# A two-layer transformer block with routed experts: the block plan and its branch ahead of the token lists, gMLP products on VectorE, and a fixed order of adds at the layers' ends

## The chip, the cores and the metric

The kernel runs on one core of a Trainium2 chip. The metric is the device time of one execution in microseconds, the median of the runs shown. Compute engines are TensorE (PE in the profile; its weight loads are PEld), VectorE (DVE), ScalarE (ACT) and GpSimd (POOL); SyncE (SP) issues most of the weight transfers.

## The reference, cut to what matters

512 latent tokens and 256 context tokens of width 1024 pass two layers. Layer 0 mixes tokens by windowed attention, layer 1 by a chunked gMLP; each is followed by a norm, a mixture of 16 experts (two per token, both of one group of four experts), and a second norm. The residual stream stays in float32.

```python
# layer 1's mixer
z = gelu(h @ w_in + b_in); u, v = z[..., :1024], z[..., 1024:]
v = layer_norm(v, ln_g, ln_b).reshape(B, n, 128, 8, 128)
s = einsum("gpq,bnqgc->bnpgc", w_s, v) + b_s
y = (u * s.reshape(B, L, 1024)) @ w_out
x = layer_norm(ALPHA * x + g_a * y, ...)
# after either mixer, for h = modulate(x, sh_f, sc_f)
s = sigmoid(h @ router_w)             # 16 scores per token; the best two of the best group
y[t] = sum over the two: gate * (silu(h @ w1[e]) * (h @ w3[e])) @ w2[e]
x = layer_norm(ALPHA * x + g_f * y, ...)
```

The modulation vectors (shift, scale and gate, twice per layer) come from a product of silu(c) with a 1024 x 6144 matrix per layer.

## The kernel before, in words

Weights stream from memory in pieces of 128 x 1024 floats, 512 KB each. One list, `pieces`, holds them in the order of use; `issue(n)` asks for all of them up to place n on the SP queue, into one pool of 28 buffers (`slot`); `adv` after each use moves `issue` on. The planner that orders the instructions of each engine works with estimated times; it takes program order as priority, may place a step ahead of others written before it, and is told otherwise by `issue_after`, by `high_priority` (what stands inside goes first) and by `in_order` (the steps of the named engines keep the order in which they are written).

The kernel's stages follow one another: modulation vectors and projections, attention, output projection with norm and routing (`mix_out`, `route`), the first MoE (`moe(0, ...)`), the last norm of layer 0, the gMLP, `mix_out` and `route` of layer 1, the second MoE, and the last norm with the stores of the output.

A MoE stage works on units: blocks of 128, 64 or 32 rows of one expert, 28 in layer 0 and 22 in layer 1, in groups of 128 rows. The first two experts of each layer are fixed (the last two of the 16), so their 24 pieces are asked for ahead; the order of the other 14 depends on the counts of tokens. `plan` (L860 to L898) ranks the experts by their counts and writes the numbers into `R["int"]`, from which SP reads where to fetch from (`fetch`, L224). It also counts the blocks that don't fit (`R["int"][:, NR:]`): `more` reads that count into a register of every engine and branches around an overflow part. `places` and `slots` make lists of tokens by one-hot columns on VectorE (L997) and small matmuls (L974); `gather` fetches the rows of one group by such a list from the GpSimd queue (L1008), and `to_xT` transposes them on TensorE (L1019). A unit is then `gemm1` (L1045), `glu` (L1055, L1056), `to_hT` (L1065), `gemm2` (L1078), and `store`, which writes the scaled rows to memory (`ydr`). At unit n - 2 `collect` gathers, for each token tile, its two rows from `ydr` (L1116). The last two units don't pass through memory: their rows reach the tokens by a matmul with one-hot columns (`rows` in `last_norm`, L695).

In `moe` the order around the change is: list and gather of group 0, plan, places, lists of groups 1 to 3, gathers 1 and 2, the branch (`more`), transposes of group 0, units. `combine` (L1124) adds the gathered rows to the residual stream: X = y * gate + X, on 128 x 1024 tiles, all four tiles of the second choice in the last unit and all four of the first behind it. `last_norm` then adds the matmuls' rows with row sums (L703), squares on ScalarE (L710) and takes a Newton square root (`newton`, L737 to L753) for two tiles at a time. In layer 0 the normalised tiles go to `pre` (transposes at L1341) and into the gMLP's v half (`vhalf`, `vnorm`), then a loop over eight column blocks f for u; there the second half of layer 1's modulation matrix (16 pieces of "mt", rows 32 to 47) is multiplied in `gemt`, two pieces per f. In this loop every other product is on VectorE (L368) and the rest on GpSimd with a ScalarE sum (L370, L371). At the kernel's end ScalarE scales, VectorE multiplies with the norm's g, GpSimd or VectorE adds b, and SP stores. Weights that are used as two float32r halves (`KSPLIT`) are split by a ScalarE cast (L229) and a VectorE subtraction (L230).

## Time and profile before

| | |
|---|---|
| median of 3 runs | 1188.14 us (1185.77 to 1191.42) |
| the profiled execution | 1186.24 us |
| its span, first to last instruction | 1184.4 us |
| PE / PEld busy | 1014.6 us (86%) / 589.6 us (50%) |
| DVE / ACT / POOL busy | 611.5 us (52%) / 359.9 us (30%) / 271.2 us (23%) |
| mean granted TensorE clock | 0.925 |
| DMA | 330.62 MB, mean 279 GB/s |

Busy times are sums of an engine's instructions; matmul ends are modelled, so a busy PE need not be at its peak. The page's 40 slices (29.6 us each) give the course: the first MoE fills slices 13 to 22, the second 30 to 38 (counted from 0).

```
PE   5799899996992999999999399599929999999980
DVE  1798988785457621221122896876565121221247
POOL 0044333323000123231213251410001221120131
PEclk7799999998996999999999799799959999999995
DMA  9934457547274999999998316365449999898991
```

### The profile page before, as it was taken

What the parts mean: (1) busy time and instruction counts of PE and PEld (TensorE: products, weight loads), DVE (VectorE), ACT (ScalarE), POOL (GpSimd) and SP (SyncE); (2) the same over time, 40 slices, a digit from 0 to 9 for tenths busy, and PEclk for the clock granted to TensorE, in tenths of its full rate; (3) what the DMA queues carried; (4) which work ended last, traced back from release to release, by engine and by line L of the source; (5) the groups of instructions that cost most, each with busy time, mean ns of one, the idle gap of its engine ahead of it and who ended that gap; (6) DMA issues with size and microseconds to landing.
All of it is one profiled execution on the core that took longest, in us unless ns stands there. A gap on an engine that the chain in (4) does not pass through costs nothing. (4 is left out here: it accounts for less than half of the span.)

```text
span 1184.4 us, 18461 instructions
## 1 busy us (share of the span) xinstructions
PE 1014.6 (86%) x6596; PEld 589.6 (50%) x6596; DVE 611.5 (52%) x1548; ACT 359.9 (30%) x730; POOL 271.2 (23%) x262
## 2 busy tenths in 40 slices
PE   5799899996992999999999399599929999999980
PEld 2577665554782444444443178488713342444420
DVE  1798988785457621221122896876565121221247
ACT  1553487775312111111121343442212110111103
POOL 0044333323000123231213251410001221120131
PEclk7799999998996999999999799799959999999995
DMA  9934457547274999999998316365449999898991
GB/s 346 408 148 174 157 196 258 173 145 256 102 269 160 377 409 390 410 410 409 410 386 324 118 46 244 131 212 203 178 189 387 410 411 410 311 407 352 386 382 71
DMA packets 104284, 330.62 MB, mean 279 GB/s; under 512 B 13346, under 2 KB 24306, under 8 KB 104179
## 3 DMA queue, kind: packets, MB, share of 16 engines
q1 hardware_dynamic: 88608, 287.56, 63.4%
q0 software_dynamic: 10848, 26.75, 6.0%
q10 hardware_dynamic: 4722, 14.98, 3.5%
q8 instruction: 56, 0.92, 0.3%
q14 instruction: 50, 0.40, 0.1%
HBM read 310.72 MB, written 21.67 MB: 281 GB/s over the span
## 5 line engine op out<-in xcount | busy, mean ns | idle before, releaser
L1045 PE MATMUL pb<-ring,xt 128*32 128x256 f32 (+1 forms) x2112 | 228.1, 440 | 1.1 <-DMA ring<-in_moe 0.8
L1045 PEld LDWEIGHTS pb<-ring,xt 128*32 128x32 f32 (+1 forms) x2112 | 86.7, 117 | 114.9 <-issue 70.4
L1089 POOL DMA_DIRECT2D ydr<-ys x132 | 67.0, 513 | 319.2 <-DVE ys L1084 258.9
L1056 DVE TENSOR_TENSOR si<-si,pb 128x128 f32<-128x128 f32 (+1 forms) x46 | 16.1, 350 | 206.9 <-ACT si L1055 203.4
L370 POOL TENSOR_TENSOR raw<-raw,row 128x1024 f32<-128x1024 f32 x32 | 90.8, 2850 | 131.8 <-DMA raw<-in_mt 104.5
L1078 PE MATMUL pb<-ring,hh 128*32 128x256 f32 (+1 forms) x1056 | 119.5, 441 | 1.7 <-ACT hh L1067 0.8
L368 DVE SCALAR_TENSOR_TENSOR raw<-raw,row 128x1024 f32<-128x1024 f32 x48 | 83.6, 1760 | 4.1 <-DMA row<-sdr 4.1
L1055 ACT ACTIVATE si<-pb 128x128 f32<-128x128 f32 (+1 forms) x46 | 15.1, 329 | 219.4 <-PE pb L1045 219.4
L1078 PEld LDWEIGHTS pb<-ring,hh 128*32 128x32 f32 (+1 forms) x1056 | 43.0, 117 | 62.5 <-issue 45.8
L1084 DVE TENSOR_TENSOR ys<-pb,gfs 128x256 f32<-128x256 f32 (+1 forms) x42 | 22.6, 537 | 81.5 <-PE pb L1078 79.9
L1008 POOL DMA_INDIRECT xg<-hdr,Rgi x22 | 23.3, 1057 | 178.6 <-DVE pq L887 87.7
L230 DVE TENSOR_TENSOR wl<-raw,wh 128x1024 fp32r<-128x1024 f32 x44 | 53.8, 1247 | 15.3 <-ACT wh L229 15.2
L1067 ACT COPY hh<-pt 128x128 f32<-128x128 f32 (+2 forms) x50 | 17.0, 339 | 146.1 <-PE pt L1065 139.4
L569 DVE TENSOR_SCALAR_CACHE_REDUCE P<-pa,nsink 128x512 f32<-128x512 f32 (+1 forms) x64 | 50.5, 809 | 19.7 <-PE pa L565 10.9
L1045 PE MATMUL pa<-ring,xt 128*128 128x512 f32 x128 | 59.4, 604 | 0.6 <-DVE xt L1027 0.6
L571 ACT ACTIVATE P<-P,nm 128x512 f32<-128x512 f32 (+1 forms) x64 | 49.5, 775 | 11.9 <-DVE P L569 11.6
L605 ACT COPY PT<-pt 128x512 f32<-128x512 f32 x72 | 39.4, 582 | 27.2 <-PE pt L604 27.0
L604 PE MATMUL pt<-cc,P 128*128 128x128 f32 x288 | 43.9, 281 | 4.1 <-ACT PT L605 3.5
L229 ACT CAST wh<-raw 128x1024 fp32r<-128x1024 f32 x44 | 44.5, 1044 | 8.7 <-DMA mdr<-gr 6.9
L604 PEld LDWEIGHTS pt<-cc,P 128*128 128x128 f32 x288 | 31.0, 141 | 31.0 <-issue 25.2
L1025 ACT ACTIVATE xt<-pt,bc,gc 128x128 f32<-128x128 f32 x88 | 33.1, 457 | 38.2 <-PE pt L1019 20.9
L614 PE MATMUL pb<-PT,Vt 128*64 128x512 f32 x144 | 38.8, 617 | 3.6 <-ACT PT L605 3.6
(368 smaller groups left out, 2005.0 us busy)
## 6 DMA issues: line engine op xcount, KB each, us to landing
ring<-in_moe SPq DMA_DIRECT2D x336, 512.0 KB
raw<-in_mt SPq DMA_DIRECT2D x80, 512.0 KB
raw<-in_moe SPq DMA_DIRECT2D x48, 512.0 KB
raw<-in_mod SPq DMA_DIRECT2D x16, 512.0 KB
raw<-in_qkv SPq DMA_DIRECT2D x12, 512.0 KB
ydr<-zero SPq DMA_DIRECT2D x10, 512.0 KB
ydr<-ys POOLq DMA_DIRECT2D x36, 128.0 KB, 5.6
raw<-in_wo SPq DMA_DIRECT2D x8, 512.0 KB
```

Of the source, the lines that this page charges most:

```text
L229: SC.copy(hi, src)
L230: V.tensor_sub(lo, src, hi.bitcast(F32))
L368: V.scalar_tensor_tensor(w, w, 1.0, srow[0], op0=OP.mult, op1=OP.mult, accum_out=mv[l][:, j:j + 1])
L370: GP.tensor_mul(w, w, srow[0])
L569: V.tensor_scalar(P[j], reg, -0.125, nsink[:, p * 8 + j:p * 8 + j + 1], op0=OP.mult, op1=OP.min, accum_out=nm[:, j:j + 1])
L571: SC.activation(P[j], P[j], AF.Exp, bias=nm[:, j:j + 1], scale=-1.0, accum_out=sums[:, j:j + 1])
L604: PE.transpose(pt[:, j * 128:(j + 1) * 128], P[a * 4 + j][:, i * 128:(i + 1) * 128], idf)
L605: cp = SC.copy(tl[:, a, :], pt)
L614: m.append(PE.matmul(po[a * 64:(a + 1) * 64, :], Vt[kb // 3][:, kb % 3, g * 64:(g + 1) * 64], tl[:, a, :], start=(i == 0), stop=(i == nb - ...
L1045: PE.matmul(o.rearrange("p (m c) -> p m c", m=2), xt[:, k, c:c + n], w[:, h], start=(k == 0), stop=(k == 7), skip_group_check=True)
L1078: PE.matmul(o, ht[f], w[:, h], start=(f == 0), stop=(f == 3), skip_group_check=True)
L1089: GP.dma_start(ydr[row:row + n, h * n * 8:(h + 1) * n * 8], ys[h * n:h * n + n, :])
```

## The change

1. `moe`: the plan stands under `high_priority`; `places`, the lists of groups 1 to 3 and the gathers 1 and 2 stand behind the branch and behind the transposes of group 0.
2. Pieces: winv 0 to 3 come ahead of the last 16 pieces of the first MoE, and are split at unit n - 2; `issue` looks 4 pieces further from the 160th on.
3. gMLP: all late products of `gemt` are on VectorE, behind the norm of v's last tile, spread by LATE over f = 1 to 7; their row (`srow`) is loaded right behind the first MoE.
4. `last_norm`: written out in a fixed order on TensorE, VectorE and ScalarE. The first choice's rows of tiles 2 and 3 are added by matmuls with a diagonal matrix of gates instead of `combine`; `combine` takes a range of tiles. Layer 0 takes the first pair's norm ahead of the last tile's sums; layer 1 takes one norm for four tiles, multiplies with g ahead of it, and works on VectorE alone, but for tile 1, whose last step is a matmul onto b with a diagonal of scales.

```diff
-    pieces += moe_pieces(0)
-    pieces += [("winv", j) for j in range(8)] + [("ws",)]
+    first = moe_pieces(0)
+    pieces += first[:-16] + [("winv", j) for j in range(4)] + first[-16:]
+    pieces += [("winv", j) for j in range(4, 8)] + [("ws",)]
+    LATE = [0, 0, 3, 6, 8, 10, 12, 14, 16]
     for j in range(8):
-        pieces += [("winu", j), ("mt", 1, 32 + 2 * j), ("mt", 1, 33 + 2 * j)]
+        pieces += [("winu", j)] + [("mt", 1, 32 + i) for i in range(LATE[j], LATE[j + 1])]
...
-    def gemt(l, j):
+    def gemt(l, j, past=None):
         w = raw("mt", l, j)
-        if (j % 4 != 3 if l and j < 32 else j % 2):
-            V.scalar_tensor_tensor(w, w, 1.0, srow[0], op0=OP.mult, op1=OP.mult, accum_out=mv[l][:, j:j + 1])
+        if past or (j % 4 != 3 if l else j % 2):
+            m = V.scalar_tensor_tensor(w, w, 1.0, srow[0], op0=OP.mult, op1=OP.mult, accum_out=mv[l][:, j:j + 1])
+            if past:
+                after(m, past)
...
+        def scaled(u, p):
+            V.scalar_tensor_tensor(ys[u], p, R["gs"][:, u:u + 1], gf, op0=OP.mult, op1=OP.mult)
+            for t in range(4):
+                rows(t, u, ys[u])
         with in_order(PE, V, SC):
...
+            scaled(0, R["py"])
+            combine(l, 1, X, 0, 2)
+            scaled(1, py)
+            for t in (2, 3):
+                for n in range(2):
+                    PE.matmul(o[t][n], dg[t - 2], R["y", t, 0][:, n * 512:n * 512 + 512], start=False, stop=True)
+            combine(l, 1, X, 2, 4)
+            combine(l, 0, X, 0, 2)
+            finish(X, sums, norm, nmu)
...
         xg[0] = gather(R["gi"][:, 0:1])
-        places, rows, gates = plan(l)
-        places()
-        listed = slots(l, 1, 4)
-        for g in (1, 2):
-            xg[g] = gather(R["gi"][:, g:g + 1])
+        with tc.high_priority():
+            places, rows, gates = plan(l)
...
         xt = {0: to_xT(l, xg[0])}
+        places()
+        listed = slots(l, 1, 4)
+        for g in (1, 2):
+            xg[g] = gather(R["gi"][:, g:g + 1])
...
-                    issue(first + done[0] + LOOK)
+                    issue(first + done[0] + LOOK + (0 if l or done[0] < 160 else 4))
...
+            if i == n - 2 and not l:
+                for q in [("winv", j) for j in range(4)]:
+                    issue(pos[q] + 1)
+                    pairs[q] = split(raws[q])
...
+    def middle(X, sums, norm, nmu):
+        def pair(t):
+            y = norm(t, t + 2)
...
+        for t in range(3):
+            sums(t)
+        pair(0)
+        sums(3)
+        pair(2)
...
-        for j in range(2):
-            gemt(1, 32 + 2 * f + j)
+        for j in range(LATE[f], LATE[f + 1]):
+            gemt(1, 32 + j, normed)
...
+    def end(X, sums, norm, nmu):
...
+        def scaled(t):
+            V.scalar_tensor_tensor(z[t], X[t], nmu[:, t:t + 1], g2, op0=OP.add, op1=OP.mult)
+        def done(t, y):
+            V.scalar_tensor_tensor(z[t], z[t], y[:, t:t + 1], b2, op0=OP.mult, op1=OP.add)
+            SP.dma_start(out[0, t * 128:(t + 1) * 128, :], z[t])
+        for t in range(4):
+            sums(t)
...
+        scaled(0)
+        scaled(1)
+        y = norm(0, 4)
+        V.tensor_scalar(dg, idf, y[:, 1:2], None, op0=OP.mult)
+        for ns in halves:
+            PE.matmul(p[:, ns], dg, z[1][:, ns], start=False, stop=True, skip_group_check=True)
+        done(0, y)
+        for ns in halves:
+            SC.copy(o[:, ns], p[:, ns])
+        SP.dma_start(out[0, 128:256, :], o)
+        for t in (2, 3):
+            scaled(t)
+            done(t, y)
```

## Rows read from the trace of the kernel before

**Rows 1.** Windows: stretch, busy us by engine, clock, DMA share, GB/s
```profile
371.00:377.00 6.00, 0.86 (x5) 0.52 (x5) 6.00 (x27) 0.00 (x0) 1.19 (x1) 0.50 0.25 63
...
400.00:450.00 50.00, 48.83 (x424) 20.24 (x420) 19.38 (x51) 6.93 (x20) 9.26 (x16) 1.00 1.03 408
```

**Rows 2.** Timeline, routing to experts, layer 0: start, length, engine, line, count
```profile
366.90 0.22 DVE L847 SCALAR_TENSOR_TENSOR Rsel<-rrk,rwn 128x64 bf16<-128x64 f32 x1
...
369.37 0.16 DVE L867 SCALAR_TENSOR_TENSOR pcu<-pb,cc 128x14 f32<-128x14 f32 x1
...
371.66 1.19 POOL L1008 DMA_INDIRECT xg<-hdr,Rgi  x1 [60.60 <-DVE pq L877]
...
374.47 0.16 DVE L891 TENSOR_TENSOR pov<-pb,pcb 128x16 f32<-128x16 f32 x1
...
376.32 1.52 DVE L997 TENSOR_SCALAR oh<-iotab,pkr 128x32 bf16<-128x32 bf16 x10
...
379.32 0.14 DVE L898 CAST pint<-pno 128x1 int32<-128x1 f32 x1
...
384.53 1.94 PE L1019 MATMUL pt<-cc,xg 128*128 128x128 f32 x8 [5.33 <-DVE Rgi L982]
...
385.26 16.81 SPq L224 DMA_DIRECT2D ring<-in_moe  x15
...
386.75 15.00 PE L1045 MATMUL pb<-raw,xt 128*64 128x512 f32 x64 [0.28 <-DVE xt L1027]
```

**Rows 3.** Timeline of the same place in layer 1
```profile
868.36 0.23 DVE L847 SCALAR_TENSOR_TENSOR Rsel<-rrk,rwn 128x64 bf16<-128x64 f32 x1
...
886.86 20.87 SPq L224 DMA_DIRECT2D ring<-in_moe  x17
```

**Rows 4.** Waits, PEld, 886 to 960 us: total us, times, longest
```profile
PEld pb L1045 <- DMA ring<-in_moe: 6.3, 7, 1.1
```

**Rows 5.** DMA issues: median us from issue to landing
```profile
xg<-hdr,Rgi POOLq DMA_INDIRECT x22, 8.2
```

**Rows 6.** Timeline, end of the first MoE
```profile
646.10 2.03 POOL L1116 DMA_INDIRECT y<-ydr,prow  x1 [0.30 <-PE pb L1078]
...
659.18 3.79 DVE L1124 SCALAR_TENSOR_TENSOR x<-y,pg,x 128x1024 f32<-128x1024 f32 x3 [1.43 <-DMA y<-ydr,prow]
...
674.49 1.97 PE L1341 MATMUL pt<-cc,x 128*128 128x128 f32 x8 [17.35 <-ACT x L1374]
```

**Rows 7.** Timeline, the gMLP around its gap
```profile
737.96 14.55 POOL L370 TENSOR_TENSOR raw<-raw,row 128x1024 f32<-128x1024 f32 x5 [3.51 <-DMA row<-sdr]
...
750.27 2.26 DVE L748 SCALAR_TENSOR_TENSOR cnu<-cny,cnv 128x1 f32<-128x1 f32 x1
...
754.94 1.22 PE L1419 MATMUL pt<-raw,v 128*128 128x128 f32 x4 [11.68 <-ACT v L1370]
...
762.29 1.22 DVE L368 SCALAR_TENSOR_TENSOR raw<-raw,row 128x1024 f32<-128x1024 f32 x1
```

**Rows 8.** Windows in the gMLP
```profile
755.00:765.00 10.00, 8.77 (x26) 6.64 (x27) 8.71 (x13) 6.62 (x11) 1.03 (x1) 0.55 0.60 198
...
765.00:770.00 5.00, 5.00 (x24) 4.12 (x23) 4.31 (x9) 2.43 (x5) 1.37 (x1) 1.00 0.34 104
...
765.00:810.00 45.00, 45.00 (x237) 38.28 (x236) 33.90 (x44) 23.96 (x34) 6.16 (x3) 1.00 0.60 201
```

**Rows 9.** Timeline, the kernel's end
```profile
1145.51 6.50 DVE L1124 SCALAR_TENSOR_TENSOR x<-y,pg,x 128x1024 f32<-128x1024 f32 x5 [0.81 <-DMA y<-ydr,prow]
...
1161.33 0.20 DVE L715 TENSOR_SCALAR xv<-xq 128x1 f32<-128x1 f32 x1
...
1164.69 2.37 ACT L1439 ACTIVATE x<-x,xm,xny 128x1024 f32<-128x1024 f32 x2 [1.73 <-DVE xm L723]
...
1177.93 2.35 DVE L1441 TENSOR_TENSOR x<-x,row 128x1024 f32<-128x1024 f32 x2
```

**Rows 10.** Groups of instructions, 1150 to 1185 us: busy us, mean ns
```profile
L703 DVE SCALAR_TENSOR_TENSOR x<-pa,x 128x512 f32<-128x512 f32 x4 | 2.6, 687 | 0.1
```

More of the change, by code (lines that the diff above doesn't have):

```diff
@@ L240, in ensure_split @@
                     return
-            else:
+            elif p not in pairs:
                 issue(nsplit[0] + 1)
@@ L686, in last_norm @@
         q = small([128, 4, 2], F32, "xq", 1)
-        v = [small([128, 3, 2], F32, "xv") for _ in range(2)]
+        v = small([128, 3, 4], F32, "xv", 1)
         o = [psA(), psA(), psT(), psT()]
         o = [[o[0][:, :512], o[0][:, 512:]], [o[1][:, :512], o[1][:, 512:]], o[2:], [psB(), psB()]]
-        ys = slot([128, 512], F32, "ys")
+        ys = [slot([128, 512], F32, "ys") for _ in range(2)]
+        dg = [tt2([128, 128], F32, "dg") for _ in range(2)]
+        for i in range(2):
+            SC.activation(dg[i], idf, AF.Identity, scale=R["g"][:, 0, 2 + i:3 + i])
         def rows(t, u, y):
@@ L695, in rows @@
                 PE.matmul(o[t][n], R["oT"][n * 64:n * 64 + 64, u, t * 128:(t + 1) * 128], y[n * 64:n * 64 + 64, :],
-                          start=(u == 0), stop=(u == 1))
-        for t in range(4):
-            rows(t, 0, R["yp"])
+                          start=(u == 0), stop=(u == 1 and t < 2))
         def add(t, n):
@@ L1118, in collect, with combine @@
                                   bounds_check=ZR[l], oob_is_err=False)
-    def combine(l, a, X):
+    def combine(l, a, X, t0, t1):
         R = RT[l]
-        for t in range(4):
+        for t in range(t0, t1):
             V.scalar_tensor_tensor(X[t], R["y", t, a], R["g"][:, a, t:t + 1], X[t], op0=OP.mult, op1=OP.add)
@@ L1317, in hybrid_kernel @@
     binv = load_row(A["binv"], alloc=uslot)
+    srow[0] = load_row(sdr, alloc=uslot)
     X = X0
@@ L1369, in vnorm @@
         rstd, nmr = ln_stats(v, "c")
-        SC.activation(v, v, AF.Identity, bias=nmr, scale=rstd)
-    for t, (y, nmr) in zip((0, 2), last_norm(0, X, py, gf)):
-        for i in range(2):
-            SC.activation(X[t + i], X[t + i], AF.Identity, bias=nmr[:, i:i + 1], scale=y[:, i:i + 1])
+        return SC.activation(v, v, AF.Identity, bias=nmr, scale=rstd)
+    def middle(X, sums, norm, nmu):
+        def pair(t):
+            y = norm(t, t + 2)
+            nmr = small([128, 2], F32, "xm")
+            V.tensor_mul(nmr, nmu[:, t:t + 2], y)
+            for i in range(2):
+                SC.activation(X[t + i], X[t + i], AF.Identity, bias=nmr[:, i:i + 1], scale=y[:, i:i + 1])
+        for t in range(3):
[3 more added lines that the diff above has]
+        pair(2)
+    last_norm(0, X, py, gf, middle)
     with in_order(V, SC):
@@ L1433, in hybrid_kernel @@
     b2 = load_row(A["ln2_b"][1:2, :])
-    for t, (y, nmr) in zip((0, 2), last_norm(1, X, py, gf)):
-        for i in range(2):
-            x = X[t + i]
-            SC.activation(x, x, AF.Identity, bias=nmr[:, i:i + 1], scale=y[:, i:i + 1])
-            V.tensor_mul(x, x, g2)
-            (GP if t == 0 else V).tensor_add(x, x, b2)
-            SP.dma_start(out[0, (t + i) * 128:(t + i + 1) * 128, :], x)
+    def end(X, sums, norm, nmu):
+        z = [slot([128, D], F32, "z") for _ in range(4)]
+        o = slot([128, D], F32, "z")
+        dg = tt2([128, 128], F32, "dg")
+        def scaled(t):
[5 more added lines that the diff above has]
+            sums(t)
+        p = psA()
+        halves = [slice(n * 512, n * 512 + 512) for n in range(2)]
+        for ns in halves:
+            PE.matmul(p[:, ns], idf, b2[:, ns], start=True, stop=False, skip_group_check=True)
+        scaled(0)
[5 more added lines that the diff above has]
+        done(0, y)
+        for ns in halves:
+            SC.copy(o[:, ns], p[:, ns])
[3 more added lines that the diff above has]
+            done(t, y)
+    last_norm(1, X, py, gf, end)
 def host_arrays(inputs):
```

41 lines of the change are left out of this document (14 added, 27 removed).

## The prediction, made before the changed kernel was run

> **What bounds the kernel now.** I read the windows first, then the order of time around the places that the diff touches, then the waits. In a MoE stage [rows 1] TensorE is busy for 48.83 of 50 us at full clock while the DMA engines are full at 408 GB/s: both limits touch, so nothing inside the stage is worth much, and what counts is when the stage starts. The reader should then look at four places where neither is busy: the route to the first expert of each layer, the end of the first MoE, the gMLP, and the last 40 us.
>
> **Before the experts.** The routing's last step, Rsel, ends at 367.12 [rows 2]. The plan of blocks needs nothing else, yet its first VectorE step (L867) comes at 369.37, its middle (L891) at 374.47 and its last, the count that the branch reads (L898), at 379.32; the one-hots of groups 1 to 3 (L997, ten in 1.52 us) lie between the last two. Behind the count stands the branch: TensorE starts at 384.53, and the first expert weight whose number had to be computed is asked for at 385.26. Layer 1 has the same length from Rsel to ring [rows 3]: 18.50 us, against 18.36.
>
> After the change the plan has priority and the lists of groups 1 to 3 and their gathers come behind the branch. Step by step: L867 can start when Rsel's counts are through TensorE, about 367.8 (an estimate: 1.6 us earlier, what group 0's one-hots take in front of it); L867 to L891 stays at 5.1 us, since the steps hang on one another; the five small steps behind it take some 1.3 us without the one-hots instead of 4.85. The count is there at 374.2, 5.2 us earlier. The branch itself is not made shorter: count to ring stays at 5.9 us. Bounds: 3.5 us, if group 0's twelve list steps are woven into the plan, and 6.5 us, if none is.
>
> What this is worth differs by layer. In layer 0 TensorE hardly waits for weights once it runs [rows 1], so the gain is that of its first transpose. That needs gather 0, issued at 371.66 [rows 2]; 63 GB/s over 371 to 377 is about 378 KB [rows 1], the gather and nothing else, so it had landed by 377, at most 5.4 us after its issue, long before the branch let TensorE go. With the plan in front, group 0's list is 0 to 4 us later, the landing at 376 to 381, the branch's end at 379.3. I take 4.5 us of the 5.2. In layer 1 TensorE waits 6.3 us for ring weights in the first 74 us [rows 4], so an earlier ring also shortens that: I take 5.0.
>
> The moved lists cost nothing only as long as group 1's gather lands before TensorE has finished the first two units, 15.00 us of matmuls (L1045) from 386.75 [rows 2], then from about 382 to 397. VectorE has behind the branch: placing the tokens (an estimate of 2 us, two fifths of the 5.1 in which the plan's like steps run), 24 one-hots at 0.15, and the evictions of the first transposes with small sums, another 2: about 7.5 us, so the list ends near 387, the gather is issued at 388 and lands 8.2 us later [rows 5] at 396. It is one microsecond early: cover, but thin. Each further microsecond is a stall in both layers; the gemm2 of unit 0 can fill some. I keep 0 in the sum and 3 us per layer in the range. Twelve one-hot matmuls per layer now stand among the first unit's matmuls, and the three gathers and memsets on POOL are issued behind the branch as before.
>
> **End of the first MoE.** The y gathers are what ends last: three combines (L1124) start at 659.18 after a DMA wait, and the first transpose of the gMLP comes at 674.49, 15.3 us later [rows 6]. In the new order there follow two combines instead of four (those of tokens 2 and 3 go to TensorE as diagonal matmuls), three sums, one pair's norm and one ScalarE pass. With the prices of the other end [rows 9, 10]: 2 x 1.30 for combines, 3 x 1.5 for sums (two adds at 0.65 and a small step), 3.3 for a pair's norm (1161.33 to ScalarE's start at 1164.69), 1.2 for ScalarE: 659.2 + 11.6 = 670.8, a gain of 3.7. Against it stands the sdr row, a fifth broadcast of 512 KB at 408 GB/s, 1.3 us on the gathers' DMA. For it: the four splits of winv leave this place, and with them the slow POOL issue at 646.10 (2.03 us, where gather 0 took 1.19). I take 3.0, bounds 0 and 6. Those splits now lie beside the last two units' gating, where VectorE has room (19.38 of 50 us busy [rows 1]). The four winv weights ahead of the last 16 expert weights delay those by 4 x 1.3 us; the last unit's matmuls run well behind its weights, and LOOK grows by 4 there, so 0; if the cover is gone, 5 us.
>
> [...]
>
> **The gMLP gap.** TensorE stands still for 11.68 us before 754.94 [rows 7], waiting for the fourth row of v, whose norm on VectorE is stretched: a Newton step (L748) takes 2.26 us at 750.27 while POOL runs five products (L370) in 14.55 us. The change gives all 16 late products to VectorE, places them after that norm, and starts with f = 1. Without POOL beside it the norm's chain is about 3 us, so v is ready before the two units of matmuls that fill the time to 743 are done: the 11.7 us go. After the gap the clock is low [rows 8]: 26 matmuls in 755 to 765 at 0.55, where 765 to 770 does 24 in 5 us, so 10 us for 5.4 us of work: another 4.6. Gross 16.3 us.
>
> Its price is on VectorE. From 765 to 810 it is busy for 33.90 of 45 us [rows 8]. About 8 products more than before fall into that stretch, 1.22 us each [rows 7]: 9.8, together 43.7 of 45. That hides just so, and not where three products fall on one f. If it does not, VectorE is late with the splits of winu and wout, and TensorE waits. I take 2.8 us of waits, bounds 0 and 7: net 13.5. The products on POOL and their ScalarE sums fall away at no gain, as neither engine bounds here.
>
> **The end.** VectorE works without a break from 1145.51 to 1180.28 (the last step's start plus 2.35) [rows 9], then the last store takes 4.1 us to the span's 1184.4. New order, from the first y: 6 combines at 1.30 (7.8), one scaling 0.75, four sums 6.0, two scalings with g2 2.5, the norm of four at once 3.9 (a pair's 3.3 and two more variances), the diagonal 0.2, five passes of 1.28 (6.4): 27.6, so 1173.1 and with the store 1177.2: 7.2 us. Gone are two combines, POOL's add, and the four ScalarE passes in the chain. TensorE's new work (four diagonal matmuls, b2, the row of token 1) and ScalarE's two copies lie beside it. Bounds 4 and 9.
>
> **Sum.** 4.5 + 5.0 + 3.0 + 13.5 + 7.2 = 33.2 us off the profiled 1186.24 (span 1184.4): 1153. The runs' median is 1.9 above the profiled one, so I expect a median of 1154.
>
> **The rivals.**
> - Late lists and a full VectorE: group 1's gather comes 4 us late in both layers and the products cost 7 us instead of 2.8 in the gMLP. For it: one microsecond of cover and 97% of VectorE. Against: gemm2 fills part. 33 - 8 - 4 = 21 us: 1167.
> - The order does not come out as written. The order of instructions is planned from estimated times, and in the trace the one-hots, written behind the plan, stand in front of its last step [rows 2]. If other steps fill VectorE before the count again, the branch moves by 1 us, and 8.5 us of the sum are lost: 1162.
> - More than forecast: both MoE starts at 6 us, the gMLP without a wait, y gathers earlier: 44 us, 1144.
> - Slower than before. Place: VectorE behind the first unit's gating. If the lists of groups 1 to 3 are placed behind the residual passes of `rest` (eight of 1.22 us, as a product of that size, behind some 4 us of small steps that start when half of the 15.00 us is done, near 391), the list ends at about 409 instead of 387, the gather lands at 418, and TensorE, done with unit 1 at 397, has one gemm2 of other work, half a gemm1 or 4 us: 17 to 22 us of standing in each layer, with the clock falling as at 755. From 16.6 us per layer it eats the whole sum; at 22 with 4 for the clock the time is 1154 + 52 = 1206. For it: only the planner's order holds the lists in front. Against: the lists come first in the program, and VectorE is idle at that time.
>
> **How the numbers follow.** Forecast (1146 to 1162) 0.60; late lists and full VectorE 0.15; order not as written 0.10; more 0.08; slower 0.04; 0.03 for a gain that vanishes for reasons that I do not see. Less than 0.5% (6 us) can't be told from no change here. All but the last two are faster: 0.93; no change 0.03; slower 0.04. The range goes from the better case to past the late lists, 1142 to 1171, and leaves out some 0.12.
>
> **What would show it.** Right: L898 some 1.3 us behind L891 instead of 4.85; the ring's first issue 13 us after Rsel in both layers; no TensorE idle over 2 us before L1019's second block; transposes (L1341) 11.5 us after the first combine of a = 0; no POOL L370 in the gMLP and TensorE at full clock from vhalf to the routing; the last VectorE step 27.6 us after the first y. Wrong: TensorE idle between unit 1 and the transposes of group 1, idle for winu's or wout's splits, or a count that stays behind the one-hots.

## The result and the profile after

The changed kernel's median is 1170.39 us (1169.32 to 1173.94, four runs) against 1188.86 us (1185.77 to 1191.42, four runs): a ratio of 0.9851, 95% interval 0.9819 to 0.9883. That is 18.5 us off where the forecast had 34. The time lies inside the range of 1142 to 1171, at its edge, and outside the likeliest case's own range (1146 to 1162). The profiled execution took 1169.32 us with a span of 1167.5 us; the mean granted clock went from 0.925 to 0.945.

The page's 40 slices of the kernel after (29.2 us each); the standstill of slice 25 is gone and POOL is nearly idle there:

```profile
PE   6799799996994899999999679999928999999994
DVE  1799989876356732222112687886567121211217
POOL 0044433324000113232022241000011221221140
PEclk9999989998997899999999879999959999999997
DMA  9934447637375899999999602765479999899893
```

The two traces cut at the same events, in us (the forecast is the prediction's own term):

| stretch | before | after | saved | forecast |
|---|---|---|---|---|
| start to Rsel, layer 0 (nothing changed) | 366.90 | 368.34 | -1.4 | 0 |
| Rsel to the last gemm2 of the first MoE | 280.53 | 279.17 | 1.4 | 4.5 |
| to the first transposes of the gMLP | 27.06 | 23.44 | 3.6 | 3.0 |
| to v's end (VectorE's last addition in `vhalf`) | 55.50 | 64.48 | -9.0 | 0 |
| to Rsel, layer 1 | 138.37 | 125.40 | 13.0 | 13.5 |
| to the last gemm2 of the second MoE | 275.55 | 273.14 | 2.4 | 5.0 |
| to the span's end | 40.53 | 33.56 | 7.0 | 7.2 |
| span | 1184.4 | 1167.5 | 16.9 | 33.2 |

The first stretch is scatter: over the fourteen profiles of this study it lies between 363.4 and 370.8 us with the same work in it. Of the prediction's five terms two came out as forecast, the gMLP and the kernel's end. The two starts and the end of the first MoE did not; the last of these is the sum of two rows, since v's part was priced at nothing: 3.6 - 9.0 = -5.4 us where 3.0 were forecast. The lines behind them follow.

Layer 0 from Rsel on, the timeline of the kernel after (start, length, engine, line, operation, count, idle time before and its releaser):

```profile
368.34 0.23 DVE L860 SCALAR_TENSOR_TENSOR Rsel<-rrk,rwn 128x64 bf16<-128x64 f32 x1
...
373.10 1.20 POOL L1021 DMA_INDIRECT xg<-hdr,Rgi  x1 [62.38 <-DVE pq L890]
...
374.07 0.20 DVE L904 TENSOR_TENSOR pov<-pb,pcb 128x16 f32<-128x16 f32 x1
...
375.25 0.15 DVE L911 CAST pint<-pno 128x1 int32<-128x1 f32 x1
...
380.79 1.94 PE L1032 MATMUL pt<-cc,xg 128*128 128x128 f32 x8 [9.71 <-DVEq L1281]
381.36 27.57 SPq L226 DMA_DIRECT2D ring<-in_moe  x23
...
382.52 1.36 DVE L1040 TENSOR_SCALAR xt<-pt,gc,bc 128x128 f32<-128x128 f32 x4
...
384.24 0.19 PE L987 MATMUL pb<-aux,oh 128*128 128x4 bf16 x1 [1.51 <-DVE oh L1010]
...
384.35 8.90 PE L1058 MATMUL pb<-raw,xt 128*64 128x512 f32 x26
...
393.40 1.85 DVE L1010 TENSOR_SCALAR oh<-iotab,pkr 128x96 bf16<-128x96 bf16 x12 [7.08 <-PE pb L987]
...
398.90 1.00 POOL L1021 DMA_INDIRECT xg<-hdr,Rgi  x1 [17.27 <-DVE pm L939]
...
407.66 1.09 PE L1032 MATMUL pt<-cc,xg 128*128 128x128 f32 x8
```

Against [rows 2] the count (L911) stands 1.2 us behind L904 instead of 4.85, and the ring is asked 13.0 us after Rsel instead of 18.4. But the first matmuls (L1058) come 3.56 us after the first transposes (before: 2.22), behind a one-hot matmul (L987) that waits for VectorE, and VectorE waits 7.08 us in the middle of the lists for TensorE to read one-hots. The windows of these matmuls, busy us by engine, then the clock:

```profile
385.00:389.00 4.00, 4.00 (x12) 1.16 (x10) 1.32 (x10) 0.57 (x1) 0.00 (x0) 0.50 1.04 374
389.00:393.00 4.00, 4.00 (x16) 1.07 (x12) 0.00 (x0) 0.00 (x0) 0.00 (x0) 0.90 0.89 260
```

TensorE is busy in every one of these microseconds, in the first window at a clock of 0.50: 12 matmuls in 4 us, where the kernel before did 21 in 389 to 393 at full clock.

Layer 1, the answer to [rows 3]:

```profile
872.42 1.32 POOL L1021 DMA_INDIRECT xg<-hdr,Rgi  x1 [162.37 <-SPq L1281]
...
873.39 16.75 SPq L226 DMA_DIRECT2D ring<-in_moe  x14
...
878.15 1.94 PE L1032 MATMUL pt<-cc,xg 128*128 128x128 f32 x8
```

The ring is again early (12.6 us after Rsel; 18.5 before). The gather of group 0, however, is released by the branch itself (SPq L1281): it was placed behind it, 11.6 us after Rsel instead of 5.4. The first transposes come 17.3 us after Rsel, 0.8 earlier than before (experiment 1 shows that the gather is not all that holds them). The waits of PEld for the ring (total, times, longest; 873 to 947 us) fell from 6.3 us [rows 4] to 4.7:

```profile
PEld pb L1091 <- DMA ring<-in_moe: 2.4, 3, 1.1
PEld pb L1058 <- DMA ring<-in_moe: 2.3, 4, 1.0
```

The end of the first MoE, the answer to [rows 6]:

```profile
660.51 1.28 DVE L1137 SCALAR_TENSOR_TENSOR x<-y,pg,x 128x1024 f32<-128x1024 f32 x1 [1.26 <-DMA y<-ydr,prow]
...
670.95 1.97 PE L1356 MATMUL pt<-cc,x 128*128 128x128 f32 x8 [3.35 <-ACT x L1393]
...
673.06 2.36 POOL L1370 TENSOR_TENSOR x<-x,row 128x1024 f32<-128x1024 f32 x1 [21.53 <-PE pt L1356]
...
675.49 2.43 POOL L1371 TENSOR_TENSOR x<-x,row 128x1024 f32<-128x1024 f32 x1
675.62 2.33 DVE L754 TENSOR_SCALAR xny<-xv 128x2 int32<-128x2 int32 x1
...
681.31 2.40 POOL L1370 TENSOR_TENSOR x<-x,row 128x1024 f32<-128x1024 f32 x1 [3.39 <-issue]
...
681.93 1.80 DVE L763 TENSOR_TENSOR xnu<-xny 128x2 f32<-128x2 f32 x1
...
683.80 2.51 POOL L1371 TENSOR_TENSOR x<-x,row 128x1024 f32<-128x1024 f32 x1
683.99 2.33 DVE L764 TENSOR_TENSOR xnu<-xnu,xv 128x2 f32<-128x2 f32 x1
...
688.78 0.16 DVE L1391 TENSOR_TENSOR xm<-xn,xny 128x2 f32<-128x2 f32 x1
```

The reader should add each start and length. L754 ends at 677.95 and POOL's L1371 at 677.92; L763 at 683.73 and L1370 at 683.71; L764 at 686.32 and the last L1371 at 686.31. Steps that take 0.15 us elsewhere end when POOL's product ends. The norm of blocks 2 and 3 is there at 688.9, where the kernel before had it at 683.3, and TensorE runs dry. The kernel before paid the same price in this place, for two steps of its second chain instead of three, beside its own POOL products:

```profile
677.00 2.01 DVE L751 TENSOR_TENSOR xnu<-xnu,xv 128x2 f32<-128x2 f32 x1
...
679.26 2.33 DVE L752 SCALAR_TENSOR_TENSOR xny<-xnu,xny 128x2 f32<-128x2 f32 x1
```

The windows behind this place and in the gMLP, after the change:

```profile
690.00:700.00 10.00, 5.90 (x27) 4.51 (x26) 6.47 (x13) 4.95 (x8) 4.70 (x2) 0.85 0.00 0
700.00:790.00 90.00, 86.08 (x393) 70.07 (x392) 75.11 (x165) 34.93 (x46) 5.82 (x3) 0.98 0.55 195
...
742.00:755.00 13.00, 10.60 (x55) 8.53 (x55) 9.91 (x17) 7.32 (x9) 0.00 (x0) 1.00 0.67 255
```

In 690 to 700 TensorE is busy 5.90 us of 10 (9.91 before). From 700 on the change does what it was forecast to do: where 11.68 us stood empty [rows 7] TensorE is busy 10.60 of 13 us, and the clock stays up where it had been 0.55 [rows 8].

The kernel's end, the answer to [rows 9]:

```profile
1134.79 1.28 DVE L1137 SCALAR_TENSOR_TENSOR x<-y,pg,x 128x1024 f32<-128x1024 f32 x1 [4.33 <-DMA y<-ydr,prow]
...
1160.92 1.28 DVE L1470 SCALAR_TENSOR_TENSOR z<-z,xny,row 128x1024 f32<-128x1024 f32 x1
```

From the first y to the last VectorE step: 27.4 us (forecast 27.6).

### The profile page after: what moved, and what is told of

Read it like the earlier page. It is cut to its first block, busy times and chain, and to the rows that moved or that the text cites. A ratio compares the mean times of both kernels' runs of the same rounds, so it can differ in the third digit from the quotient of the medians.

```text
span 1167.5 us, 18483 instructions
## 1 busy us (share of the span) xinstructions
PE 1033.8 (89%) x6620; PEld 595.7 (51%) x6620; DVE 603.8 (52%) x1546; ACT 348.8 (30%) x716; POOL 240.2 (21%) x252
## 3 DMA queue, kind: packets, MB, share of 16 engines
q1 hardware_dynamic: 88608, 287.56, 64.5%
## 5 line engine op out<-in xcount | busy, mean ns | idle before, releaser
L1058 PE MATMUL pb<-ring,xt 128*32 128x256 f32 (+1 forms) x2112 | 225.8, 440 | 0.4 <-DVE ys L1097 0.2
L1058 PEld LDWEIGHTS pb<-ring,xt 128*32 128x32 f32 (+1 forms) x2112 | 87.0, 117 | 112.2 <-issue 71.5
L370 DVE SCALAR_TENSOR_TENSOR raw<-raw,row 128x1024 f32<-128x1024 f32 x56 | 89.2, 1612 | 0.0
L374 POOL TENSOR_TENSOR raw<-raw,row 128x1024 f32<-128x1024 f32 x24 | 68.1, 2847 | 100.1 <-DMA raw<-in_mt 100.1
L1058 PE MATMUL pa<-ring,xt 128*128 128x512 f32 x128 | 59.4, 604 | 0.6 <-DVE xt L1040 0.6
L1080 ACT COPY hh<-pt 128x128 f32<-128x128 f32 (+2 forms) x50 | 16.9, 338 | 142.4 <-PE pt L1078 135.8
L609 ACT COPY PT<-pt 128x512 f32<-128x512 f32 x72 | 39.4, 582 | 27.1 <-PE pt L608 26.9
L1040 DVE TENSOR_SCALAR xt<-pt,gc,bc 128x128 f32<-128x128 f32 x88 | 30.0, 404 | 31.7 <-PE pt L1032 31.7
## 6 DMA issues: line engine op xcount, KB each, us to landing
ring<-in_moe SPq DMA_DIRECT2D x336, 512.0 KB, 10.5
```

Of the source, the lines that this page charges most:

```text
L370: m = V.scalar_tensor_tensor(w, w, 1.0, srow[0], op0=OP.mult, op1=OP.mult, accum_out=mv[l][:, j:j + 1])
L374: GP.tensor_mul(w, w, srow[0])
L609: cp = SC.copy(tl[:, a, :], pt)
L1058: PE.matmul(o.rearrange("p (m c) -> p m c", m=2), xt[:, k, c:c + n], w[:, h], start=(k == 0), stop=(k == 7), skip_group_check=True)
```

## The experiments

All ratios are to the kernel before, with the 95% interval of five rounds: some 0.2 to 0.3 points to either side, so that smaller differences between two experiments are not told by the time. The stretches are read from one profiled execution each; one that no edit touched (v's end to Rsel, in the builds with the gMLP part) lies between 125.1 and 127.5 us.

### 1. The gather of group 0 in front of the branch

```diff
-        more(l, gf)
+        with tc.issue_after(last[0].ins): more(l, gf)
```

> The changed kernel with one thing more: on POOL the gather of group 0 stands ahead of the conditional block in layer 1 too (in layer 0 it does already). Theory: in layer 1 the gather, whose list is ready at 864.7, waited behind the block until 872.4, and TensorE's first transpose with it, 17.3 us after Rsel instead of some 12.5; so the first transpose should come 11.5 to 12.5 us after Rsel, the layer's last gemm2 some 4 us earlier, and the time be 1166 against the changed kernel's 1170 (ratio to the kernel before 0.981). Rival: the layer's weights decide (the ring is asked for 12.6 us after Rsel in either case): the transposes come earlier, TensorE then waits for ring weights, the end of the layer stays within 1 us, and so does the time, 1170 (0.985).

Measured: 1169.02 us, ratio 0.9845 (0.9819 to 0.9871). In layer 1 the gather is issued 6.3 us after Rsel instead of 11.6, but the first transposes come at 16.9 instead of 17.3:

```profile
866.82 1.03 POOL L1021 DMA_INDIRECT xg<-hdr,Rgi  x1 [159.18 <-DVE pnb L906]
...
876.11 0.23 PE L987 MATMUL pb<-aux,oh 128*128 128x4 bf16 x2 [12.83 <-DVE oh L1010]
...
876.64 0.19 PE L987 MATMUL pb<-aux,oh 128*128 128x4 bf16 x1 [0.29 <-DVE oh L1010]
877.06 0.48 PE L987 MATMUL pb<-aux,oh 128*128 128x4 bf16 x2 [0.23 <-DVE oh L1010]
877.45 1.94 PE L1032 MATMUL pt<-cc,xg 128*128 128x128 f32 x8
```

They stand on TensorE's queue behind five one-hot matmuls (L987), which wait for VectorE. The late gather was not the only thing in front of them: the theory fell half.

### 2. The one-hots of groups 1 to 3 in buffers of their own

```diff
-                oh = small([128, 128], BF, "oh", 6)
+                oh = small([128, 128], BF, "oh", 6) if n != 3 else big[:, i * 4 + t, :]
```

> The changed kernel, but the twelve one-hots of groups 1 to 3 lie in a tile of their own instead of six turning buffers. Theory: in layer 0 VectorE stood still for 7.1 us (386.3 to 393.4) because the seventh one-hot needs a buffer that a TensorE matmul has to free, and this matmul is queued behind 26 matmuls of the first unit; so the list ended 13 us later than before and its matmuls, and the gating of unit 0 behind the last one-hots, cost TensorE some 2 to 3 us of the 4.8 that it lost between its first matmul and unit 2. Without it the wait is gone, group 1's gather is issued near 392 instead of 398.9, unit 2 starts 2 to 3 us earlier, and the time is 1167.5 (0.982). The rest, some 1.7 us, is the low clock from 384.4 to 389.5. Rival: MoE 0 is set by its DMA: unit 2 starts earlier, but the last gemm2 of layer 0 stays where it is (279 us after Rsel) and the time at 1170 (0.985).

Measured: 1170.83 us, 0.9875 (0.9855 to 0.9894). VectorE's wait of 7.08 us is gone and group 1's gather is issued 25.4 us after Rsel instead of 30.6, yet layer 0 from Rsel to the last gemm2 takes 277.7 us, as in experiments 1 and 3 (277.8 and 278.1), which have the wait. So the wait for six buffers is not what eats layer 0's gain. Layer 1 got worse, 276.1 us (its first transposes 18.5 us after Rsel).

### 3. One norm of four tiles at the end of the first MoE

```diff
-        for t in range(3):
-            sums(t)
-        pair(0)
-        sums(3)
-        pair(2)
+        for t in range(4):
+            sums(t)
+        y = norm(0, 4)
```

> The changed kernel, but behind the first MoE all four token blocks are summed and then normed by one Newton chain of four, instead of blocks 0 and 1 first and blocks 2 and 3 in a chain of their own. Theory: that second chain runs beside POOL's products of the first blocks, where a step of 0.15 us takes 1.8 to 2.3, and is done at 688.8; blocks 2 and 3 reach TensorE 5.6 us later than before, although the first blocks come 3.5 us earlier, and vhalf ends at 734.7 instead of 729.3. With one chain ahead of POOL's products the first transpose comes 1 to 2 us later, near 672.5, the last blocks 13 us earlier, vhalf ends at 728 to 730, and the time is 1165 (0.980). Rival: VectorE, 9.1 to 9.9 of 10 us busy from 670 to 690, is full of evictions and splits in either order: vhalf ends at 734 and the time is 1170 to 1171 (0.985).

Measured: 1163.54 us, 0.9809 (0.9787 to 0.9830). From the last gemm2 to v's end 84.1 us, against 87.9 in the changed kernel and 82.6 before. The single chain of steps (0.16 to 0.17 us each) ends at 674.48, before POOL's first product starts (678.18), so nothing in it is stretched. (POOL's products still lie beside VectorE's later subtractions, as in the kernel before; without them experiment 10 takes 77.0 us here.) A side effect: the planner now placed layer 1's gather and first transposes ahead of the one-hot matmuls, and that layer took 269.8 us instead of 273.1; part of the gain may be that (experiment 8 has the same early start in layer 1, and there the layer took 274.1).

### 4. The gMLP part of the change alone

```diff
-        if (j % 4 != 3 if l and j < 32 else j % 2):
+        if past or (j % 4 != 3 if l else j % 2):
...
-            gemt(1, 32 + 2 * f + j)
+            gemt(1, 32 + j, normed)
```

> The kernel before with the gMLP part of the change alone: the late products on VectorE, from f = 1 on and placed after the fourth row's norm, and the row that they need fetched early. Theory: this part is worth what was forecast for it, 13.5 us: TensorE's wait of 11.7 us and the low clock behind it go, and VectorE's waits for the splits of winu give some 3 us back; 1175 against 1188.5 (0.989). Rival: the part was over-priced and is what went missing (half of the forecast was): 6 to 8 us, 1181 (0.994), with TensorE waiting for splits from 750 to 800.

Measured: 1173.42 us, 0.9888 (0.9869 to 0.9908): 13.3 us by the ratio; from v's end to Rsel 138.4 us became 125.1. The forecast's 13.5 stands.

### 5. The plan part alone

```diff
+        with tc.high_priority():
+            places, rows, gates = plan(l)
...
         xt = {0: to_xT(l, xg[0])}
+        places()
+        listed = slots(l, 1, 4)
```

> The kernel before with the plan part of the change alone: the plan with priority, the conditional block right behind it, the lists of groups 1 to 3 behind that. In this order of instructions POOL's gather of group 0 stands ahead of the block in both layers. Theory: in layer 0 TensorE's first matmul comes 4 us earlier after Rsel and unit 2 not at all (the four early starts that were run have it -0.6 to +1.0 us against the kernel before), since the first matmuls run at the low clock for longer and one-hot matmuls and the late eviction of group 1 stand among them: 1 to 2 us at the end of the layer; in layer 1, with gather and transposes in front, 5 us. Together 6 to 7: 1180 against 1186.4 (0.9945). Rival one, the forecast: 9.5 us, 1177 (0.992). Rival two: layer 1 gains no more than in the changed kernel, 2.5 us, and all is 4: 1182.5 (0.9965).

Measured: 1182.77 us, 0.9974 (0.9957 to 0.9990): 3.1 us instead of 9.5. Layer 0 gains 2.2 us, layer 1 3.7 (its first transposes come at 11.9 us here, but its clock is full only 10.5 us behind them); 2.1 us are missing between the last gemm2 of the first MoE and v's end, where this kernel is as before; why was not found. The small gain of this part does not come from the other parts beside it.

### 6. The gather in front, and group 0's transposes ahead of the one-hot matmuls

```diff
-                PE.transpose(pt[:, k * 128:(k + 1) * 128], xg[:, c:c + 128], idf)
+                last[0] = PE.transpose(pt[:, k * 128:(k + 1) * 128], xg[:, c:c + 128], idf)
...
-        more(l, gf)
+        with tc.issue_after(last[0].ins): more(l, gf)
...
-        listed = slots(l, 1, 4)
+        with tc.issue_after(last[0].ins): listed = slots(l, 1, 4)
```

> The changed kernel, with POOL's gather of group 0 ahead of the block and TensorE's one-hot matmuls of groups 1 to 3 behind the transposes of group 0 (in layer 1; layer 0 has this order already). Theory: in layer 1 both were in the way: with the gather alone in front, the first transpose still came 16.9 us after Rsel, behind five one-hot matmuls, whose one-hots VectorE makes only after 2 us of placing. With both the first transpose comes 12 us after Rsel, the layer's last gemm2 270 us after Rsel (changed kernel 273.1, before 275.6), and the time is 1165.5 on this chip's scale of 1186.4 for the kernel before (0.9825). Rival: ring weights decide; the layer ends 272 to 273 us after Rsel and the ratio stays at 0.985.

Measured: 1165.88 us, 0.9818 (0.9799 to 0.9836). Layer 1's first transposes come 12.1 us after Rsel, 5.2 earlier than in the changed kernel, and the layer ends 2.1 us earlier (271.0). More than half of the early start is lost again: the first matmuls come 4.9 us behind the first transposes, with one-hot matmuls between, and the clock is full only 10.5 us behind those.

### 7. POOL's products behind the norm of v

```diff
-        GP.tensor_mul(x, x, lg2)
-        GP.tensor_add(x, x, lb2)
...
+    for x in X:
+        after(GP.tensor_mul(x, x, lg2), normed)
+        GP.tensor_add(x, x, lb2)
```

> The changed kernel, but POOL's eight products and sums on the normed rows (x times ln2_g plus ln2_b, 2.4 us each), which run from 673 to 709 beside VectorE, are placed behind the last norm of v. Theory: they are what stretches VectorE's small steps (1.8 to 2.3 us for 0.15) and its subtractions (1.9 to 4.0 for 0.8 a pair), so that blocks 2 and 3 come late; without them vhalf ends 58 us after the first transpose instead of 64.5, and the time is 1163 to 1165 (0.981) as far as the products don't do the same to VectorE in the loop over f, where it is busy for 9 of 10 us. Rival one: VectorE's own work fills that time, vhalf ends where it did, 1169 (0.985). Rival two: the loop over f pays all of it back, 1169 to 1172, with vhalf early and Rsel of layer 1 not.

Measured: 1173.79 us, 0.9897 (0.9880 to 0.9914), 0.46 points behind the changed kernel's 0.9851. From the first transposes to v's end 64.5 us became 53.2: the products had cost 11.3 us there. But from v's end to Rsel 125.4 became 142.0. The two engines in the new place:

```profile
727.10 9.44 POOL L1417 TENSOR_TENSOR x<-x,row 128x1024 f32<-128x1024 f32 x4
...
729.55 2.33 DVE L765 SCALAR_TENSOR_TENSOR cny<-cnu,cny 128x1 f32<-128x1 f32 x1
731.92 2.33 DVE L761 SCALAR_TENSOR_TENSOR cnu<-cny,cnv 128x1 f32<-128x1 f32 x1
...
736.51 12.26 POOL L1418 TENSOR_TENSOR x<-x,row 128x1024 f32<-128x1024 f32 x4
...
743.22 3.35 DVE L370 SCALAR_TENSOR_TENSOR raw<-raw,row 128x1024 f32<-128x1024 f32 x1
```

and the window of that place:

```profile
730.00:750.00 20.00, 7.56 (x34) 6.13 (x32) 19.86 (x14) 4.40 (x5) 18.77 (x7) 0.72 0.39 141
```

Newton steps of 0.16 and 0.22 us take 2.33, products of 1.21 us take 3.35, VectorE is busy for 19.86 of 20 us with 14 instructions, and TensorE stands for 12.4 of them. In both of the places that were tried, POOL's products hold up the work that VectorE has beside them.

### 8. Both pairs' norms in front, still two chains

```diff
-        for t in range(3):
+        for t in range(4):
             sums(t)
         pair(0)
-        sums(3)
         pair(2)
```

> The changed kernel, but the sums of block 3 come ahead of the norm of blocks 0 and 1, so that the norm of blocks 2 and 3 follows at once, as in the kernel before. (The order of instructions in layer 1 has the gather and the transposes in front here, as in the run with one norm of four, whose layer 1 ended 269.8 us after Rsel.) Theory: with the second chain mostly ahead of POOL's products the first transpose comes 26 to 27 us after the last gemm2 (changed kernel 23.4, one norm of four 28.9) and vhalf ends 82 to 83 us after it (87.9 and 84.1; before 82.6): 5 us; with 3 us of layer 1 the time is 1161 on the scale of 1186.4 (0.979). Rival: the order of the sums does not matter since POOL's products begin at the first transpose and stretch the second chain anyway: vhalf at 87, and 1166 (0.983) for layer 1 alone.

Measured: 1163.64 us, 0.9802 (0.9780 to 0.9824). Last gemm2 to v's end 84.7 us. Its second chain still has two stretched steps (2.01 and 2.34 us) and ends 36.4 us behind the last gemm2 instead of 41.4. One norm or two makes no difference that can be told (84.1 against 84.7); how many steps fall beside the products does. The 3 us that were expected of layer 1 did not come: 274.1 us, with the clock full only 10.5 us behind the first transposes.

### 9. Lists of groups 1 to 3 behind the first unit

```diff
-        listed = slots(l, 1, 4)
-        for g in (1, 2):
-            xg[g] = gather(R["gi"][:, g:g + 1])
...
+            if i == 0:
+                with tc.issue_after(evicted), tc.issue_after(last[0].ins):
+                    listed = slots(l, 1, 4)
```

(`evicted` is the last VectorE eviction of group 0's transposes, `last` the first unit's last gemm1 matmul; with the edits of experiments 1 and 2.)

> The changed kernel, with POOL's gather of group 0 ahead of the block in both layers, the twelve one-hots of groups 1 to 3 in a tile of their own, VectorE's one-hots behind the eviction of group 0 and TensorE's one-hot matmuls behind the first unit's gemm1. Theory for the start that gave nothing: in the kernel before the first matmul follows 2.2 us after the first transpose and the clock is full 4.1 us after it; in every build with the early start a gap stands between transposes and matmuls (3.5 us in layer 0, 4.9 in layer 1), the clock is full only 7 to 11 us after the first transpose, and one-hot matmuls wait among the first unit's. Without them the first matmul comes 2 us after the first transpose, the clock is full 4 to 5 us after it, unit 2's hidden transposes stand 36 to 37.5 us after Rsel instead of 40.5 to 42 (before 41.1), and the layers end 274 to 275.5 and 267 to 269 us after Rsel (changed kernel 279.2 and 273.1, before 280.5 and 275.6): 1161 on the scale of 1186.3 (0.979). Rival: unit 2 comes early and DMA takes it back, the layers end at 277.5 and 271: 1165.5 (0.9825).

Measured: 1159.29 us, 0.9774 (0.9744 to 0.9803). Layer 0, timeline and a window:

```profile
382.94 1.94 PE L1032 MATMUL pt<-cc,xg 128*128 128x128 f32 x8 [9.63 <-DVE pq L920]
384.81 7.72 PE L1058 MATMUL pb<-raw,xt 128*64 128x512 f32 x32
...
392.47 0.45 PE L987 MATMUL pb<-aux,ohb 128*128 128x4 bf16 x12
```

```profile
387.00:391.00 4.00, 4.00 (x20) 1.26 (x18) 4.00 (x28) 0.73 (x1) 0.00 (x0) 1.00 0.98 350
```

In layer 0 the matmuls follow the transposes at once, the clock is full within 4 us of them, and the layer takes 273.9 us: 6.6 less than before, where the change gave 1.4. Layer 1 takes 268.9, 6.7 less than before, although the pause stays there: the first matmul comes 3.5 us behind the first transpose, since VectorE places tokens ahead of its evictions, and the clock is full after 7.2 us. So an early branch is worth what was forecast, and more, with the matmuls of the lists behind the first unit. How much each of this run's edits gives in layer 1 was not separated.

### 10. The products on VectorE, behind the gMLP's loop

```diff
-        GP.tensor_mul(x, x, lg2)
-        GP.tensor_add(x, x, lb2)
...
+    with tc.issue_after(i.ins):
+        for x in X:
+            V.tensor_mul(x, x, lg2)
+            V.tensor_add(x, x, lb2)
```

> The changed kernel, but the eight products and sums on the normed rows (ln2_g, ln2_b) are on VectorE, behind its last step of the gMLP's loop, where it is busy for 7.4 of 20 us (810 to 830), instead of on POOL beside the first half of v. Theory: POOL's instructions are what stretches VectorE: vhalf ends 53 us after the first transpose, as with the products late on POOL (changed kernel 64.5), the loop over f keeps its time (Rsel 125 to 127 us after vhalf, where products late on POOL made it 142), since eight steps of 1.22 us lie in VectorE's gaps between the blocks of the output: 9 us, 1160 on the scale of 1186.3 (0.9775). Rival: they delay the first blocks of the output by their full 9.8 us, Rsel comes 134 us after vhalf, and the time is 1167 (0.984).

Measured: 1161.45 us, 0.9795 (0.9767 to 0.9822). First transposes to v's end 53.1 us (64.5), v's end to Rsel 129.3 (125.4): 11.4 won, 3.9 given back: all eight passes of 1.22 us lie between 782.9 and 796.8, ahead of VectorE's first block of the output (797.8).

### 11. Experiments 9 and 10 together

```diff
+            if i == 0:
+                with tc.issue_after(evicted), tc.issue_after(last[0].ins):
+                    listed = slots(l, 1, 4)
...
+            V.tensor_mul(x, x, lg2)
+            V.tensor_add(x, x, lb2)
```

> The two edits together: lists behind unit 0 with the gather in front, and the products on VectorE behind the gMLP's loop. They lie in different stages, so the gains add: 7.5 and 9 us off the changed kernel's 1168.7 on the scale of 1186.3: 1152 (0.971). If the clock at the start of the gMLP or the order that the planner makes elsewhere changes with it, 1157 (0.975).

Measured: 1155.74 us, 0.9736 (0.9709 to 0.9764). Against the changed kernel that is 1.15 points of the ratio, where the two alone gave 0.77 and 0.56: they add up but for a small part. From v's end to Rsel it is 132.1 us, more than in experiment 10.

### 12. As experiment 11, each tile's products behind the statistics of the tile before

```diff
+                if product and not n:
+                    product(t)
...
+    def product(t):
+        with tc.issue_after((last[0] if t else i).ins):
+            V.tensor_mul(X[t], X[t], lg2)
+            V.tensor_add(X[t], X[t], lb2)
...
-                with tc.issue_after(rows().ins):
-                    rest(0, 4)
+                ranked = rows().ins
+            if i == 4:
+                with tc.issue_after(ranked): rest(0, 4)
```

> The lists behind unit 0 and the gather in front, as before; the products on VectorE one block at a time, each behind the statistics of the block before it; and the eight residual passes of `rest`, which stand between group 1's eviction and the gating of unit 1 (1.6 us of TensorE idle at 37 to 39 us after Rsel in each layer), moved from the first unit to the fifth. Theory: Rsel of layer 1 comes 126 us after vhalf (132 in the run of both edits, 125 in the changed kernel), unit 2 another 1.5 us earlier in each layer; 1155.7 - 6 - 3 = 1147 (0.966 on the scale of 1187.3). Rival: the products wait on VectorE behind each block's statistics and delay the next block's residual; nothing is won there, 1153 (0.971).

Measured: 1149.61 us, 0.9678 (0.9663 to 0.9693), faster than either kernel. From v's end to Rsel 125.0 us: nothing is given back any more. The second chain and the window after it:

```profile
673.25 0.15 DVE L763 TENSOR_TENSOR xnu<-xny 128x2 f32<-128x2 f32 x1
...
673.65 0.15 DVE L764 TENSOR_TENSOR xnu<-xnu,xv 128x2 f32<-128x2 f32 x1
...
675.07 0.16 DVE L1395 TENSOR_TENSOR xm<-xn,xny 128x2 f32<-128x2 f32 x1
```

```profile
690.00:700.00 10.00, 10.00 (x46) 8.18 (x45) 6.44 (x7) 5.35 (x7) 0.00 (x0) 1.00 0.64 236
```

No step is stretched, and TensorE is busy 10.00 of the 10 us in which the changed kernel had 5.90. The other half, the residual passes of `rest` moved from the first to the fifth unit, brought nothing: the transposes of the second unit's hidden rows come 37.2 and 40.1 us after Rsel (experiment 9: 37.1 and 39.4), and TensorE's gap of 1.6 us ahead of them stayed in both layers.

## Why the prediction had the sign right and the size wrong

**The step that failed is the term "End of the first MoE".** It was priced from the combines to the first transpose (659.2 + 11.6, "I take 3.0, bounds 0 and 6"), and that transpose did come 3.5 us earlier (670.95 against 674.49). But TensorE needs four tiles there, and the second pair's norm was priced at nothing. In the new order its chain begins after the first pair's passes and runs beside POOL's products L1370 and L1371, which start as soon as the first transposes are read. The term measured -5.4 us (3.6 - 9.0) instead of +3.0, half of what is missing, 8.4 of 16.3. Experiment 7 shows the products to be worth 11.3 us in that place, experiments 10 and 12 show that the loss goes when POOL does not run them (77.0 and 74.8 us from the last gemm2 to v's end, against 87.9 with the change and 82.6 before), experiments 3 and 8 that about 3.5 us of it go when the chain, or most of it, is put in front of them. The rows for it were at hand: the prediction itself read a Newton step of 2.26 us beside POOL's products [rows 7] and credited the gMLP with its removal, and the trace of the kernel before has two such steps in the very place that the term prices (677.00 and 679.26). In the gMLP the change took POOL away from a norm; at the end of the first MoE it started the second chain 1.9 us later (its first Newton step at 675.62 instead of 673.75) and three of its steps were caught instead of two.

The traces show how closely the two go together. In the kernel after L763 and L764 (two inputs) end within 0.02 us of POOL's products, and in experiment 7 a row of four steps of two inputs (L761 and L765) takes 2.24 to 2.33 us each beside four products of 2.36. L754, a tensor_scalar with one input, was held for 2.33 us as well and ended 0.03 us behind a product. By what means a product holds a step up, no run here shows.

**The two starts: "I take 4.5 us of the 5.2" and "I take 5.0".** The count came 5.5 to 6.1 us earlier (forecast 5.2), the ring 5.3 and 6.0. The layers gained 1.4 and 2.4. The step that failed here is "the gain is that of its first transpose". In layer 0 those did come 5.2 us earlier after Rsel. But VectorE's placing steps now stand ahead of its evictions of them (L1040 at 382.52), and a one-hot matmul that waits for VectorE stands ahead of the first unit (L987 at 384.24), so that the first matmuls come 3.56 us after the transposes instead of 2.22, and the clock stays at 0.50 until 9 us after those instead of 4, which is 21.4 us after Rsel against 21.7 before. The transposes of the second unit's hidden rows (L1078) come 42.0 us after Rsel, against 41.1 before. The length of layer 0 goes with that moment: from the full clock to the last gemm2 it is 257.1 to 259.2 us in all fourteen profiles, while the whole layer takes 273.9 to 280.5. Some of the loss is chance: with the same order of instructions in layer 0, the clock was full 6.8 to 7.5 us behind the first transposes in experiments 1, 3, 5, 6, 8 and 10, and the layer took 277.7 to 278.3 us instead of 279.2.

In layer 1 the planner put group 0's gather behind the branch, and one-hot matmuls in front of the first transposes, which came 0.8 us earlier instead of some 5. Experiment 2 acquits the six buffers as to layer 0's length, experiment 6 gives layer 1 its early transposes but not the clock, and experiment 9, with the matmuls of the lists behind the first unit, returns 6.6 and 6.7 us. In layer 1 the time from the full clock to the last gemm2 varies from 248.3 to 253.9 us, so the clock alone does not account for that layer, and the rest of its cause stays open.

**The rivals.** Late lists came true in layer 0 as to the place: group 1's gather was issued at 398.9, 11 us later than worked out, since the lists waited 7.08 us inside and stood between evictions. But TensorE had gemm2 to do and stood only 0.81 us for it; the loss lay ahead of it, in the low clock. So it is by chance that the 1167 of this rival lies near the measured time: neither of its two prices was paid. Its other half, a full VectorE in the gMLP, did not come: net 13.0 us in the change, 13.3 in experiment 4. "The order does not come out as written" came true in layer 1, not for the count but for the gather, which the prediction had not named. The slower case, lists behind `rest`, did not happen: L1322 starts at 400.80, behind the list.

**The rest.** gMLP 13.0 of 13.5; the end 7.0 of 7.2, with 27.4 us from first y to last VectorE step against 27.6; the eight y gathers, with no winv subtraction beside them any more, took 0.99 to 1.40 us each to issue, where four of the eight had taken 1.55 to 2.03 [rows 6]. No run takes this edit alone, so what the splits' place is worth is not shown. VectorE did not work quite "without a break" at the end of the kernel before: it was busy for 32.16 of the 34.77 us from 1145.51 on. And the 1.19 us of gather 0 [rows 2], which the prediction held against the 2.03 us at 646.10, lie beside the plan's tensor_tensor steps; a gather beside one-hots (385.30 in the kernel before) took 0.99 us. What makes one issue longer than another, no run here shows. By ratios the parts alone give 1.12% (gMLP) and 0.26% (plan), and 7.0 us of the trace for the end is 0.59%: 1.97% against the 1.49% measured. The 0.48% between them, 5.7 us, agrees with the 5.4 us of the first MoE's end, though each of these ratios is known to 0.2 or 0.3 points only.

## What to carry to other kernels

Where a stage hands several tiles on, price the last tile's chain, not only the first one's, and look at what the other engines start as soon as the first tile is out. Before moving a chain of small VectorE steps, list the GpSimd tensor operations that will run beside it: here each step so caught took 1.8 to 2.3 us instead of 0.15, and moving the GpSimd work to another busy place only moved the cost (11.3 us won, 16.6 lost), while giving it to VectorE, one tile at a time, removed it. An early branch gave its microseconds in both layers here only when the matmuls of the lists that had been moved behind it were held back behind the first unit (6.6 and 6.7 us, against 1.4 and 2.4): look at what stands between the branch, the first transposes and the first matmuls.

## What the runs showed of the hardware

- **The clock after the branch.** In the 28 starts of a MoE in these 14 profiles TensorE comes out of the branch at a granted clock of 0.50. In 11 of them the first matmul starts at most 2.2 us after the first transpose, which means at once behind the transposes (1.94 us); in ten of these the clock is full (1.00) 3.1 to 4.1 us after the first transpose, in one (experiment 11, layer 0) 6.1 us after it. In the other 17 the matmuls start 3.1 to 4.9 us after it, and the clock is full after 6.8 to 10.5 us. What sets the length within the second group was not settled; it is not the order of the instructions alone, since eight profiles with the same order in layer 0 have 6.8 to 9.3 us.
- **The engines left the branch one after another.** In layer 0 of the kernel after, behind the count at 375.40 ScalarE's first instruction starts at 376.5, POOL's at 378.0, VectorE's at 380.6, and the ring is asked at 381.4. What sets these distances, no run here shows.
